# Small experts in shared passes of the array: raw float32 weights on two or four column tiles

## The chip, the cores and the metric

The kernel runs on one core of a Trainium2 chip. The metric is the device time of one execution in microseconds. Inside a profile, times are counted from the first instruction of the span.

## What is computed

Two transformer blocks follow one another on 256 tokens of width 1024, all in float32. The second ends in a mixture of 64 experts, and only that part is touched here. A router picks 8 experts for each token; an expert multiplies its tokens by a gate and an up matrix, and the product of both by a down matrix:

```python
def expert_block(args):
    x_b, g_b = args
    hg = jnp.einsum('td,edf->tef', x_b, w_gate)      # 1024 -> 256, for each expert
    hu = jnp.einsum('td,edf->tef', x_b, w_up)
    return jnp.einsum('tef,efd->td', jax.nn.silu(hg) * hu * g_b[..., None], w_down)
```

An expert has 6 blocks of 128 x 1024 numbers (512 KB): 4 of gate and up together, 2 of down.

## The kernel before

`moe` first computes the router and the shared expert, then orders the experts by their number of tokens (rank 0 has most). It works on 50 ranks; what is beyond their slots is left to a branch behind the outputs (`tc.If`), entered only if a count in `more` is over its limit. The 16 ranks up to `HEAVY` get 128 token slots each; the 34 up to `LIGHT` come in pairs with 64 slots each. One heavy rank or one pair is a unit, and `run` goes through 33 units, heavy and light in turn, two units to a group. The instruction order of SP, TensorE, VectorE and ScalarE is that of the program text.

For a unit u, `run` does this in order:

- Four or eight steps of gate/up, each with one block. In between TensorE turns the result h of the unit before (`turn`), gathers tokens of the next group by products with one-hot matrices (`gather`, tile pga, copied to xg by ScalarE), and makes the tables of a later group (`select`, `tables`, tile pv).
- `swiglu` on ScalarE and VectorE.
- `combine` of unit u - 2: its output, split in two parts, times a one-hot matrix, into four accumulators.
- The down product of unit u - 1 (`dn_block`), with float32 weights just as they were loaded. For a pair the two experts have 64 columns of the array each.

In gate/up a number is the sum of two float32r parts. `load` brings a block into one of 13 raw buffers, taken in turn; ScalarE makes its high part and VectorE the low part (`split`), in six pairs of buffers, and the raw buffer is free again. A heavy unit uses 3 products per chunk of 128 inputs (`gu_block`). A pair uses `gu_block2`: an expert's 64 slots stand twice in xg, high parts above low ones, so that the array holds one expert with both parts stacked, and 2 products per chunk give halves that `swiglu` adds. So the two experts of a pair go through the array one after the other.

`ahead` traces loads so that four gate/up blocks lie ahead of the products; SP issues them in that order, each when its raw buffer is free.

Of the kernel before, what the change touches and what calls it, by code (L numbers as in the profile page):

```python
# [11 lines left out]
F32 = mybir.dt.float32  # L12
# [120 lines left out]
def norm_rows(e, pool, x, g, out):  # L133
    """out = x * rsqrt(mean(x^2) + eps) * g for [128, 1024] (g on all partitions)."""
# [8 lines left out]
def block1_mix(e, a, x, begin):  # L143
    """a: dict of APs; x: two [128, 1024] residual tiles, updated in place; begin()(t, half) is told when a part is done."""
# [20 lines left out]
    # q, k of the neighbourhood attention, transposed: [2 heads x 64, tokens]  # L165
# [13 lines left out]
    def moving(blks, width, per):  # L179
        """Columns with the tokens on partitions: psum tiles for the two halves."""  # L180
# [16 lines left out]
    def attention(pair, q_of, k_of, v_of, bias_of, dst):  # L197
        """Two heads: softmax(q k^T / 8 + bias) v, as [2 x 64, tokens]."""
# [63 lines left out]
    # q, k, v of the grouped attention  # L262
# [17 lines left out]
    for tt, qk in enumerate(qks):  # L280
# [4 lines left out]
        # rotation: halves of 16 within each section of 32  # L285
# [28 lines left out]
    # gates  # L314
# [39 lines left out]
    for nh in range(2):  # L354
# [6 lines left out]
        else:  # L361
            # the first tokens' sums end before the second's
# [30 lines left out]
    # window [r2, c, h, v, c']: rpb[h, v + 5 - r2, c' - c + 15]  # L393
# [33 lines left out]
def peer_norm(e, a, x, s):  # L427
    """The norm of x, transposed in s.xT: returns the function that takes on half of x[t]."""
# [25 lines left out]
def peer(e, a, x, s, side, after, finish):  # L454
    """side(): work of a later part to trace between the last experts; after(): buffers; finish(tail, load) what comes after all but
    the last products, which tail(t, half) does for a part of x.

    x += product-key experts of rmsnorm(x); every expert's row is used densely, gated by G."""
# [10 lines left out]
    # constants  # L469
# [7 lines left out]
    # queries, scores, the best 16 keys of each half  # L477
# [33 lines left out]
    def route():  # L511
# [11 lines left out]
        # the best 16 sums of each head: only pairs (a, b) with (a + 1)(b + 1) <= 16 can be among them  # L523
        for tt in range(2):
# [30 lines left out]
            # expert numbers of the chosen pairs  # L555
# [14 lines left out]
            # gates  # L570
# [67 lines left out]
    def mix(steps, side, share):  # L638
        """Trace the steps with work of the side queue between them, share us of it per step."""
# [68 lines left out]
    # the first tokens' sums end before the second's  # L708
# [75 lines left out]
def norm_mod(e, pool, x, A, sh, out):  # L784
    """out = x * rsqrt(mean(x^2) + eps) * A + sh."""
# [4 lines left out]
def mixer_constants(e, a, m):  # L790
    """What the start of the mixer needs."""
# [12 lines left out]
    # lower bounds: softmax over the two rows, first row  # L804
# [18 lines left out]
def mixer_start(e, a, x, m, tail, load_w):  # L823
    """x += the last sums, x = rmsnorm(x) * gf, the modulated norm of that, transposed, in m.hT, and HGRN2's f in m.pf."""
# [63 lines left out]
    # what the mixer loads next, four blocks ahead of the products  # L888
# [24 lines left out]
def mixer(e, a, x, m):  # L913
    """x += g1 * token_mixer(h) for the h in m.hT."""
# [32 lines left out]
    def moving(blks, src, lhs, name="pmv", per=4):  # L947
        """The tokens on partitions; per blocks at a time for one half of the tokens and then the other."""
# [49 lines left out]
    def conv_all(starts):  # L998
        """Each one's end after the next one's start."""
# [8 lines left out]
    # ---- HGRN2's f; beta and the log decay of each head, tokens on partitions; k  # L1008
# [23 lines left out]
    # softplus(z) = max(z, 0) - ln(sigmoid(|z|))  # L1032
# [38 lines left out]
    # ---- gated delta rule over the whole sequence  # L1071
# [6 lines left out]
    def delta():  # L1078
# [44 lines left out]
        # R = (I + N)^-1 for the strictly upper N, by doubling the inverted blocks  # L1123
# [125 lines left out]
    # ---- outputs, gated  # L1249
# [11 lines left out]
    # from here on the order of the trace is the order of each engine  # L1261
# [66 lines left out]
def turned(e, h, q, tt, dst_hi, dst_lo):  # L1328
    """Four chunks of h from q on, transposed and rounded; returns what traces the low parts."""
# [8 lines left out]
def out_block(e, m, tt, i):  # L1338
    """A block of the output projection, of w_out's columns in m.w into m.po."""
# [43 lines left out]
NE = 64  # L1383
HEAVY = 16
LIGHT = 50
# [28 lines left out]
def moe(e, a, x, m, late, out):  # L1414
    """x += the rest of the mixer's output; out = rms_norm(x + g2 * moe(modulated norm of x)) * final_norm_w."""
# [7 lines left out]
    def add_to(t, p, n, g):  # L1423
        """x += g * p for a column half."""
# [5 lines left out]
    # ---- the rest of the mixer's output projection, the norm, the shared expert's first product, the router  # L1430
# [61 lines left out]
    # silu(x wg) * (x wu) * gate, times wd, of 128 tokens of an expert, or of 64 each of two  # L1492
# [7 lines left out]
    def gu_block2(pg, xx, b, w):  # L1500
        """Rows 64 and on have the tokens' low part."""
        for k in range(2):
            c = 2 * b + k
            s = slice(k * 512, (k + 1) * 512)
            for r in range(2):
                nc.tensor.matmul(pg, xx[:, c], w[r][:, s], start=c == 0 and r == 0, stop=c == NC8 - 1 and r == 1)  # L1506

    def swiglu(pg, gt=1.0):
        h = wk.tile([P, 256], F32, tag="eh", name=uid(e, "hh"))
        if len(pg) == 2:  # L1510
            s = wk.tile([P, 512], F32, tag="t5", name=uid(e, "hs"))
# [4 lines left out]
        else:  # L1516
            s = pg[0]
        nc.scalar.activation(h, s[:, :256], AF.Silu)
        nc.vector.scalar_tensor_tensor(h, h, gt, s[:, 256:], op0=OP.mult, op1=OP.mult)
# [19 lines left out]
    # ---- shared expert, routing  # L1539
# [60 lines left out]
    hsh.append(turn(swiglu([pg[0]])))  # L1600
# [379 lines left out]
```

## Time and profile before

| | |
|---|---|
| runs | 1849.41 us median of 3 (1847.86 to 1853.87) |
| span of the profiled execution | 1846.2 us |
| its own time | not listed beside its span |
| mean granted TensorE clock | 0.981 |
| PE, DVE, ACT, POOL busy | 94%, 77%, 55%, 10% |
| HBM read | 385.74 MB |

The span is the time from the first to the last instruction of one execution. Matmuls are pipelined and their ends are modelled, so that the distance between the starts of two products says more than the length of one.

### The profile page before, as it was taken

To read this page: it belongs to the slowest core of one execution; us is meant where nothing else is said; L and a number is where in the kernel's file an instruction comes from. 1 tells how busy PE (TensorE), PEld (TensorE's weight loads), DVE (VectorE), ACT (ScalarE), POOL (GpSimd) and SP (SyncE) were. 2 spreads that over 40 slices of the span, in tenths; PEclk is the share of its full clock that TensorE was granted. 3 is DMA by queue.
4 is the path that set the end of the run, shared out by engine and by line. 5 is a ranking of instruction groups with operands and counts; after the bars stand their busy time and mean duration, and the time that the engine had idled before them with its cause. 6 is when DMAs were issued, how large, how long until landed. Compare 5 with 4: busy or idle time off the path is not lost.

```text
span 1846.2 us, 30513 instructions
## 1 busy us (share of the span) xinstructions
PE 1739.2 (94%) x11079; PEld 1461.8 (79%) x11079; DVE 1416.0 (77%) x2574; ACT 1023.9 (55%) x1782; POOL 192.5 (10%) x95
## 2 busy tenths in 40 slices
PE   7989898999999999998999989989889999999996
PEld 6779797999899998877777779878667776777774
DVE  5675799986889999777777676886767777877766
ACT  3556454444444444554544555564467777777774
POOL 1030001232111221000000020240200000000000
PEclk9999999999999999999999999999999999999998
DMA  6323544455445555788888554320478988989884
GB/s 232 115 92 127 171 149 156 153 186 169 139 137 162 172 173 170 241 276 283 275 270 278 178 171 144 130 92 1 141 297 303 364 312 320 353 317 354 320 317 186
DMA packets 107551, 388.87 MB, mean 211 GB/s; under 512 B 12592, under 2 KB 12880, under 8 KB 107264
## 3 DMA queue, kind: packets, MB, share of 16 engines
q1 hardware_dynamic: 105552, 382.48, 59.1%
q0 software_dynamic: 976, 2.82, 0.5%
q8 instruction: 89, 1.46, 0.3%
q10 hardware_dynamic: 864, 1.53, 0.3%
q14 instruction: 70, 0.57, 0.1%
HBM read 385.74 MB, written 1.05 MB: 210 GB/s over the span
## 4 chain that ended last, share of the span: by engine, by line
PE 65%; DVE 17%; DMA 10%; ACT 4%; issue 3%; POOL 0%; DVEq 0%; SPq 0%; ACTq 0%
PE acc L682 7%; PE pgu L1506 7%; PE py L1534 7%; DMA raw<-in_w_ada 6%; PE pgu L1498 5%; PE pu L80 5%; PE pu L82 5%; PE pu L81 5%; DVE wlo L67 4%; PE py L1777 3%; PE pga L1761 3%; DMA raw<-in_peer_v 2%; ACT whi L66 2%; PE pg L628 2%; PE pmv L81 1%
## 5 line engine op out<-in xcount | busy, mean ns | idle before, releaser
L66 ACT ACTIVATE whi<-raw 128x1024 fp32r<-128x1024 f32 x537 | 565.8, 1067 | 359.2 <-PE pu L81 141.3
L67 DVE TENSOR_TENSOR wlo<-raw,whi 128x1024 fp32r<-128x1024 f32 x481 | 589.1, 1234 | 159.0 <-ACT whi L66 136.8
L82 PE MATMUL pu<-pxT,wlo 128*128 128x256 f32 x1024 | 290.7, 284 | 10.1 <-DVE wlo L67 7.3
L682 PE MATMUL acc<-whi,hh 128*128 128x512 f32 x1008 | 281.9, 397 | 13.5 <-DVE hh L67 11.0
L80 PE MATMUL pu<-pxT,whi 128*128 128x256 f32 x1024 | 293.4, 286 | 0.7 <-ACT whi L66 0.7
L81 PE MATMUL pu<-pxT,whi 128*128 128x256 f32 x1024 | 290.2, 283 | 0.0
L682 PEld LDWEIGHTS acc<-whi,hh 128*128 128x128 f32 x1008 | 187.1, 188 | 64.8 <-DVE hh L67 20.9
L67 POOL TENSOR_TENSOR wlo<-raw,whi 128x1024 fp32r<-128x1024 f32 x56 | 151.6, 2710 | 661.9 <-ACT whi L66 658.5
L82 PEld LDWEIGHTS pu<-pxT,wlo 128*128 128x128 f32 x1024 | 196.6, 192 | 12.0 <-DVE wlo L67 8.9
L80 PEld LDWEIGHTS pu<-pxT,whi 128*128 128x128 f32 x1024 | 196.6, 192 | 0.9 <-ACT whi L66 0.9
L81 PEld LDWEIGHTS pu<-pxT,whi 128*128 128x128 f32 x1024 | 196.7, 192 | 0.0
L682 PE MATMUL acc<-wlo,hh 128*128 128x512 f32 x504 | 157.2, 392 | 3.0 <-DVE wlo L67 3.0
L66 ACT ACTIVATE hh<-H 128x256 fp32r<-128x256 f32 x126 | 52.5, 417 | 145.4 <-PE acc L682 144.7
L1534 PE MATMUL py<-raw,th 128*64 128x512 f32 (+1 forms) x348 | 117.0, 598 | 1.5 <-ACT xg L1768 0.9
L682 PEld LDWEIGHTS acc<-wlo,hh 128*128 128x128 f32 x504 | 94.9, 189 | 24.0 <-DVE wlo L67 3.8
L1506 PE MATMUL pgu<-whi,xg 128*128 128x512 f32 x272 | 109.2, 401 | 0.0
L1506 PE MATMUL pgu<-wlo,xg 128*128 128x512 f32 x272 | 106.9, 393 | 0.0
L1768 ACT ACTIVATE xg<-pga 128x128 fp32r<-128x128 f32 (+1 forms) x400 | 95.9, 335 | 15.2 <-PE pga L1761 12.9
L762 DVE SCALAR_TENSOR_TENSOR ada<-raw,cs,ada 128x1024 f32<-128x1024 f32 x48 | 61.6, 1284 | 55.3 <-DMA raw<-in_w_ada 55.2
L1498 PE MATMUL pgu<-whi,xg 128*128 128x512 f32 x256 | 94.9, 421 | 1.9 <-ACT whi L66 1.9
L1761 PE MATMUL pga<-S,hs 128*128 128x256 f32 (+1 forms) x544 | 85.8, 286 | 0.0
L1761 PEld LDWEIGHTS pga<-S,hs 128*128 128x128 f32 x544 | 78.6, 190 | 7.2
(579 smaller groups left out, 3298.6 us busy)
## 6 DMA issues: line engine op xcount, KB each, us to landing
raw<-in_w_gu SPq DMA_DIRECT2D x171, 512.0 KB, 6.5
raw<-in_peer_u SPq DMA_DIRECT2D x128, 512.0 KB, 3.6
raw<-in_peer_v SPq DMA_DIRECT2D x128, 512.0 KB, 4.6
raw<-in_w_dn SPq DMA_DIRECT2D x83, 512.0 KB, 8.1
raw<-in_w_ada SPq DMA_DIRECT2D x48, 512.0 KB, 4.4
ada<-in_w_gu SPq DMA_DIRECT2D x29, 512.0 KB, 6.8
raw<-in_w_in_a SPq DMA_DIRECT2D x24, 512.0 KB, 3.5
raw<-in_w2a SPq DMA_DIRECT2D x17, 512.0 KB, 4.3
```

The costliest lines, as they stand in the source:

```text
L66: e.nc.scalar.activation(hi, src, AF.Copy)
L67: (eng or e.nc.vector).tensor_sub(lo, src, hi.bitcast(F32))
L80: nc.tensor.matmul(out, lh, rh, start=first, stop=False)
L81: nc.tensor.matmul(out, lh, rl, start=False, stop=False)
L82: nc.tensor.matmul(out, ll, rh, start=False, stop=last)
L682: nc.tensor.matmul(acc[tt][n], h[l][:, s], w[r][:, n * 512:(n + 1) * 512], start=j == order[0] and i == 0, stop=j == order[-1] and i == 2)
L762: nc.vector.scalar_tensor_tensor(mod[n], w, cs[:, c:c + 1], mod[n], op0=OP.mult, op1=OP.add)
L1498: nc.tensor.matmul(pg, l[:, c], w[r][:, s], start=c == 0 and j == 0, stop=c == NC8 - 1 and j == 2)
L1506: nc.tensor.matmul(pg, xx[:, c], w[r][:, s], start=c == 0 and r == 0, stop=c == NC8 - 1 and r == 1)
L1534: nc.tensor.matmul(py[q][t], th[:, k, t], w[i][:, q * 512:(q + 1) * 512], start=k == 0, stop=last and k == 1)
L1761: nc.tensor.matmul(p[:, k, :m], hs[i][:, tt, s], S[:, tt].rearrange("p u n -> p (u n)")[:, :m], start=tt == 0, stop=tt == 1)
L1768: nc.scalar.activation(t, p[:, :, o:o + P // n], AF.Copy)
```

## The change

- `MID` = 30: the ranks 16 to 29 come in 7 pairs with 64 slots each, the ranks 30 to 49 in 5 fours with 32 slots each. With 16 heavy units that makes 28 units. Heavy units form groups of two, and pairs and fours form groups of two (pair and four, five times, then two pairs); `sorted` mixes both kinds of group.
- Gate/up of pairs and fours takes the raw float32 blocks, without a split: `gu_shared` gives each expert of the unit its own columns of the array (64 or 32) and its own rows of one accumulator. xg holds these tokens once, as float32: `gather` adds up both parts in the accumulator.
- A step of such a unit takes 2 or 4 blocks, one per expert, and the order of loads within a unit goes by block and then by expert.
- `swiglu` has one accumulator and adds no halves. `select` is one comparison per unit. `tables` multiplies each expert's slots by float32 numbers of its own (V has no parts any more).
- The branch behind the outputs has one case more.

```diff
+MID = 30
-    def gu_block2(pg, xx, b, w):
+    def gu_shared(pg, xx, b, ws):
+        n = P // len(ws)
         for k in range(2):
             c = 2 * b + k
-            s = slice(k * 512, (k + 1) * 512)
-            for r in range(2):
-                nc.tensor.matmul(pg, xx[:, c], w[r][:, s], start=c == 0 and r == 0, stop=c == NC8 - 1 and r == 1)
+            for i, w in enumerate(ws):
+                t = slice(i * n, (i + 1) * n)
+                nc.tensor.matmul(pg[t], xx[:, c, t], w[:, k * 512:(k + 1) * 512], start=c == 0, stop=c == NC8 - 1)
...
     def swiglu(pg, gt=1.0):
-        if len(pg) == 2:
-            s = wk.tile([P, 512], F32, tag="t5", name=uid(e, "hs"))
-            nc.scalar.activation(s[:64], pg[0][64:], AF.Copy)
-            nc.scalar.activation(s[64:], pg[1][:64], AF.Copy)
-            nc.vector.tensor_add(s[:64], s[:64], pg[0][:64])
-            nc.vector.tensor_add(s[64:], s[64:], pg[1][64:])
...
-    V = pool.tile([P, 2, NE // 2, 6], F32R, name="V")
+    V = pool.tile([P, 2, NE, 2], F32, name="V")
...
-                    order += [(which, k, r) for r in units[v][0] for k in range(n)]
+                    order += [(which, k, r, len(units[v][0]) > 1) for k in range(n) for r in units[v][0]]
...
-                ready.append(load(src[bass.ds(v + b, 1)].rearrange("o p n -> (o p) n"), which == 1))
+                ready.append(load(src[bass.ds(v + b, 1)].rearrange("o p n -> (o p) n"), which == 1 or shared))
-        def weights():
-            taken[0] += 1
-            return ready[taken[0] - 1]
+        def weights(n):
+            while len(ready) < taken[0] + n:
+                ahead(len(ready) - taken[0] + 1)
+            taken[0] += n
+            return ready[taken[0] - n:taken[0]]
...
-                for i, r in enumerate(ranks):
-                    for tt in range(2):
-                        nc.vector.tensor_scalar(S[:, tt, u, i * n:(i + 1) * n], io1[:, base:base + n],
-                                                pos[:, tt, r:r + 1], None, op0=OP.is_equal)
+                nc.vector.tensor_tensor(S[:, :, u].rearrange("p t (r s) -> p t r s", r=n),
+                                        io1[:, None, None, base:base + P // n].to_broadcast([P, 2, n, P // n]),
+                                        pos[:, :, r:r + n, None].to_broadcast([P, 2, n, P // n]), op=OP.is_equal)
...
-                    nc.tensor.matmul(pv[:, u], S[:, tt, u], V[:, tt, ranks[0] // 2], start=tt == 0, stop=tt == 1)
+                    for i, r in enumerate(ranks):
+                        t = slice(i * w, (i + 1) * w)
+                        nc.tensor.matmul(pv[t, u], S[:, tt, u, t].bitcast(F32), V[:, tt, r], start=tt == 0, stop=tt == 1)
...
+            if len(us[0][0]) == 1:
+                c, i = 2 * (q // 2), q % 2
+                for k in range(2):
+                    pick(k, c + k, [i])
+                nc.scalar.activation(xg[:, c:c + 2, :n, i], p[:, :, :n], AF.Copy)
+            else:
+                pick(0, q, range(2))
+                nc.scalar.activation(xg[:, q, :n], p[:, 0, :n], AF.Copy)
...
-            steps = 4 * len(ranks)
-            for b in range(steps):
+            for b in range(4):
                 if u < len(units):
-                    if len(ranks) == 1:
-                        gu_block(pg[0], xx[:, :, :P], xx[:, :, P:], b, weights())
+                    if n == 1:
+                        gu_block(pg, xx[:, :, 0], xx[:, :, 1], b, *weights(1))
                     else:
-                        gu_block2(pg[b // 4], xx[:, :, b // 4 * P:(b // 4 + 1) * P], b % 4, weights())
+                        gu_shared(pg, xx, b, weights(n))
...
+    one, two, four = shared_by(1, 0, HEAVY, 0), shared_by(2, HEAVY, MID, 0), shared_by(4, MID, LIGHT, 0)
+    mixed = [u for k in range(len(two)) for u in (two[k:k + 1] + four[k:k + 1])]
+    kinds = [[us[i:i + 2] for i in range(0, len(us), 2)] for us in (one, mixed)]
+    order = sorted(((j + 0.5 - 0.2 * k) / len(gs), g) for k, gs in enumerate(kinds) for j, g in enumerate(gs))
+    units = [u for _, g in order for u in g]
     run(units, psh)
```

## Rows read from the trace of the kernel before

**Rows 1.** The page, part 1: busy time of each engine.

```profile
PE 1739.2 (94%) x11079; PEld 1461.8 (79%) x11079; DVE 1416.0 (77%) x2574; ACT 1023.9 (55%) x1782; POOL 192.5 (10%) x95
```

**Rows 2.** Busy time by engine, window of the routed experts; then clock, DMA share, GB/s.

```profile
1351.88:1830.30 478.42, 473.42 (x2246) 338.66 (x2246) 348.34 (x498) 355.30 (x758) 0.00 (x0) 1.00 0.85 325
```

**Rows 3.** The chain that ended last, in order of time: start, length, what.

```profile
1482.19 2.04 PE pgu L1506 x8
...
1492.22 1.97 PE py L1777 x8
...
1507.11 3.58 PE py L1534 x16
1510.69 2.04 PE pgu L1506 x8
...
1539.19 2.04 PE pgu L1506 x8
...
1826.69 3.63 PE py L1534 x16
```

**Rows 4.** Windows of 10 us among the experts, columns as in rows 2.

```profile
1355.00:1365.00 10.00, 7.88 (x32) 5.83 (x32) 5.86 (x5) 7.81 (x21) 0.00 (x0) 0.83 1.03 413
...
1405.00:1415.00 10.00, 10.00 (x43) 7.05 (x43) 9.10 (x15) 7.15 (x14) 0.00 (x0) 1.00 1.02 411
...
1475.00:1485.00 10.00, 10.00 (x52) 6.30 (x51) 5.93 (x8) 6.25 (x16) 0.00 (x0) 1.00 0.56 193
```

**Rows 5.** Waits of SP's queue, 1345 to 1800: total, times, longest.

```profile
SPq L1401 <- PE py L1534: 192.0, 34, 9.7
```

**Rows 6.** TensorE in order of time, first unit: start, length, idle before.

```profile
1351.88 0.48 PE L1498 MATMUL pgu<-whi,xg 128*128 128x512 f32 x1
...
1356.35 0.49 PE L1498 MATMUL pgu<-whi,xg 128*128 128x512 f32 x1 [1.89 <-ACT whi L66]
1357.61 0.80 PE L1498 MATMUL pgu<-wlo,xg 128*128 128x512 f32 x1 [0.76 <-DVE wlo L67]
```

**Rows 7.** TensorE in order of time, start of a light unit's gate/up.

```profile
1510.62 0.50 PE L1506 MATMUL pgu<-whi,xg 128*128 128x512 f32 x1
1510.96 0.40 PE L1506 MATMUL pgu<-wlo,xg 128*128 128x512 f32 x1
1511.20 0.39 PE L1506 MATMUL pgu<-whi,xg 128*128 128x512 f32 x1
1511.43 0.40 PE L1506 MATMUL pgu<-wlo,xg 128*128 128x512 f32 x1
```

**Rows 8.** TensorE in order of time: down products of two light units.

```profile
1480.31 0.59 PE L1534 MATMUL py<-raw,th 128*64 128x512 f32 x1
1480.32 0.59 PE L1534 MATMUL py<-ada,th 128*64 128x512 f32 x1
1480.74 0.59 PE L1534 MATMUL py<-raw,th 128*64 128x512 f32 x1
...
1506.48 0.63 PE L1777 MATMUL py<-yl,St 128*128 128x512 f32 x2
1507.04 3.65 PE L1534 MATMUL py<-raw,th 128*64 128x512 f32 x16
```

**Rows 9.** TensorE in order of time: table products and what follows.

```profile
1491.72 0.50 PE L1739 MATMUL pv<-V,S 128*128 128x6 f32 x4
1492.08 0.71 PE L1777 MATMUL py<-yh,St 128*128 128x512 f32 x2
```

**Rows 10.** Groups by line and shape, from 1200 on: count, busy us, mean ns.

```profile
L67 DVE TENSOR_TENSOR wlo<-raw,whi 128x1024 fp32r<-128x1024 f32 x182 | 218.7, 1224 | 73.4 <-ACT whi L66 52.1 <-PE py L1777 13.7 <-DMA raw<-in_w_gu 1.5
L66 ACT ACTIVATE whi<-raw 128x1024 fp32r<-128x1024 f32 x191 | 200.7, 1086 | 5.5 <-DMA raw<-in_w_gu 5.1 <-PE pmv L82 0.3
```

**Rows 11.** SP in order of time: issues of the first experts' blocks.

```profile
1344.14 5.82 SPq L1401 DMA_DIRECT2D raw<-in_w_gu  x8
```

More of the change, by code (lines that the diff above doesn't have):

```diff
@@ L1658, in moe @@
         nc.vector.tensor_scalar(lst[:, k], pl[:, 0], (4.0, 2.0)[k], None, op0=OP.mult)
-    more = pool.tile([1, 4], F32, name="more")
-    nc.vector.tensor_scalar(more[:, 0:1], pl[:, 1, 0:1], -128.0, 0.0, op0=OP.add, op1=OP.max)
-    nc.vector.tensor_scalar(more[:, 1:2], pl[:, 1, HEAVY:HEAVY + 1], -64.0, 0.0, op0=OP.add, op1=OP.max)
-    nc.vector.tensor_copy(more[:, 2:3], pl[:, 1, LIGHT:LIGHT + 1])
-    nc.vector.tensor_reduce(more[:, 3:4], more[:, 0:3], axis=AX.X, op=OP.max)
-    moreu = pool.tile([1, 4], U32, name="moreu")
+    more = pool.tile([1, 5], F32, name="more")
+    for k, (r, n) in enumerate(((0, 128.0), (HEAVY, 64.0), (MID, 32.0), (LIGHT, 0.0))):
+        nc.vector.tensor_scalar(more[:, k:k + 1], pl[:, 1, r:r + 1], -n, 0.0, op0=OP.add, op1=OP.max)
+    nc.vector.tensor_reduce(more[:, 4:5], more[:, 0:4], axis=AX.X, op=OP.max)
+    moreu = pool.tile([1, 5], U32, name="moreu")
     nc.vector.tensor_copy(moreu, more)
@@ L1743, in tables @@
-            for u, (ranks, base) in enumerate(us):
+            for u in range(n):
                 nc.vector.tensor_scalar(St[:, u], iot, sv[:, u, 0:1], None, op0=OP.is_equal)
-                c = 1 + ranks[0] % 2
-                if len(ranks) == 2:
-                    nc.vector.tensor_copy(sv[64:, u, 1:2], sv[64:, u, 2:3])
-                gt.append(sv[:, u, c:c + 1])
-            xg = pool.tile([P, NC8, 2, T], F32R, tag="xg", name=uid(e, "xg"), bufs=2)
-            return S, St, gt, xg, us
+            if len(us[0][0]) == 1:
+                xg = pool.tile([P, NC8, 2, 2, P], F32R, tag="xg", name=uid(e, "xg"), bufs=2)
+            else:
+                xg = pool.tile([P, NC8, 2, P], F32, tag="xg", name=uid(e, "xg"), bufs=2)
@@ L1752, in gather @@
+            return S, St, [sv[:, u, 1:2] for u in range(n)], xg, us
         def gather(g, q):
             S, xg, us = g[0], g[3], g[4]
-            m = len(us) * P
-            c, i = 2 * (q // 2), q % 2
-            p = ps.tile([P, 2, T], F32, tag="att", name=uid(e, "pga"), bufs=e.att_bufs)
-            for k in range(2):
-                s = slice((c + k) * P, (c + k + 1) * P)
-                for tt in range(2):
-                    nc.tensor.matmul(p[:, k, :m], hs[i][:, tt, s], S[:, tt].rearrange("p u n -> p (u n)")[:, :m],
-                                     start=tt == 0, stop=tt == 1)
@@ L1763, in gather, with pick @@
-            for u, (ranks, _) in enumerate(us):
-                n = len(ranks)
-                for j in range(n):
-                    o = u * P + j * 64
-                    t = xg[:, c:c + 2, u].rearrange("p c (s i n) -> p c s i n", s=n, i=2)[:, :, j, i]
-                    nc.scalar.activation(t, p[:, :, o:o + P // n], AF.Copy)
+            n = len(us)
+            p = ps.tile([P, 2, 2, P], F32, tag="att", name=uid(e, "pga"), bufs=e.att_bufs)
+            def pick(k, c, parts):
+                steps = [(i, tt) for i in parts for tt in range(2)]
+                for i, tt in steps:
+                    nc.tensor.matmul(p[:, k, :n].rearrange("p u n -> p (u n)"), hs[i][:, tt, c * P:(c + 1) * P],
+                                     S[:, tt, :n].rearrange("p u n -> p (u n)"), start=(i, tt) == steps[0],
+                                     stop=(i, tt) == steps[-1])
@@ L1798, in run @@
                     todo = [(new, q) for q in range(4 if u > 1 else 0, 8)] if i else [(new, q) for q in range(4)]
-                ranks, xx = units[u][0], cur[3][:, :, i]
-                pg = [ps.tile([P, 512], F32, tag="tr", name=uid(e, "pgu"), bufs=e.tr_bufs) for _ in ranks]
+                n, xx = len(units[u][0]), cur[3][:, :, i]
+                pg = ps.tile([P, 512], F32, tag="tr", name=uid(e, "pgu"), bufs=e.tr_bufs)
             def fetch(n=1):
@@ L1832, in run @@
                 py = down()
-                w = [weights() for _ in range(2 * len(units[u - 1][0]))]
+                n = len(units[u - 1][0])
                 for k in range(2):
-                    dn_block(py, th, k, w[k::2])
+                    dn_block(py, th, k, weights(n))
                 yh = wk.tile([P, D], F32R, tag="yh", name=uid(e, "yh"), bufs=1)
@@ L1865, in final, with shared_by @@
                 nc.sync.dma_start(out[tt * P:(tt + 1) * P, s], o[:, s])
-    heavy = [((r,), 0) for r in range(HEAVY)]
-    light = [((r, r + 1), 0) for r in range(HEAVY, LIGHT, 2)]
-    units = []
-    while heavy or light:
-        units += heavy[:1] + light[:1]
-        heavy, light = heavy[1:], light[1:]
+    def shared_by(n, lo, hi, base):
+        return [(tuple(range(r, r + n)), base) for r in range(lo, hi, n)]
+    one, two, four = shared_by(1, 0, HEAVY, 0), shared_by(2, HEAVY, MID, 0), shared_by(4, MID, LIGHT, 0)
[3 more added lines that the diff above has]
+    units = [u for _, g in order for u in g]
     run(units, psh)
@@ L1879, in moe @@
     if e.overflow:
-        with tc.If(nc.values_load(moreu[:, 3:4], min_val=0, max_val=T) > 0):
-            v = [nc.values_load(moreu[:, k:k + 1], min_val=0, max_val=T) for k in range(3)]
+        with tc.If(nc.values_load(moreu[:, 4:5], min_val=0, max_val=T) > 0):
+            v = [nc.values_load(moreu[:, k:k + 1], min_val=0, max_val=T) for k in range(4)]
+            with tc.If(v[3] > 0):
+                run(shared_by(2, LIGHT, NE, 0))
             with tc.If(v[2] > 0):
-                run([((r, r + 1), 0) for r in range(LIGHT, NE, 2)])
+                run(shared_by(2, MID, LIGHT, 32))
             with tc.If(v[1] > 0):
-                run([((r, r + 1), 64) for r in range(HEAVY, 32, 2)])
+                run(shared_by(2, HEAVY, MID, 64))
             with tc.If(v[0] > 0):
-                run([((r,), P) for r in range(HEAVY)])
+                run(shared_by(1, 0, HEAVY, P))
             final()
```

34 lines of the change are left out of this document (15 added, 19 removed).

## The prediction

> **What bounds the kernel now.** I read the page first: TensorE is busy for 94% of the span, the other engines are not [rows 1]. The change touches only the routed experts, so I cut the span at them. From the first gate/up product (1351.88) to the last down product, 478.4 us pass, in which TensorE is busy for 473.4, VectorE and ScalarE for about 350 each, and the DMA engines for 85% [rows 2]. The chain of waits then shows that the end is set inside this stage by TensorE alone: piece after piece is PE, and the same pair of units, one heavy and one light, comes round every 28.50 us (1482.19, 1510.69, 1539.19) [rows 3]. So TensorE time taken out of a unit comes off the total, until something else is late. What is late next is seen in windows of 10 us: the DMA engines move 411 to 413 GB/s while they have buffers to fill, and are busy for only 0.56 of a window when they have not [rows 4]; SP then waits for down products to give buffers back, 192 us in all [rows 5]. A block of 0.524 MB at 411 GB/s takes 1.276 us, and the 50 experts have 300 blocks, so the weights alone need 383 us. The change doesn't alter a byte of that.
>
> **Price of a unit before.** A light unit: gate/up, gathers and tables from 1482.19 to 1492.22 are 10.03, its combine 1.97, its down product 3.58 (1507.11 to 1510.69): 15.58. A heavy unit has the rest of 28.50: 12.92 [rows 3]. 16 heavy and 17 light give 471.6; the stage took 478.4, so 7 us go, at the start, where TensorE waits 1.89 and 0.76 for a split [rows 6] and the granted clock of a window reads 0.83 [rows 4].
>
> **Gate/up of the light experts.** Removed: 32 float32r products of a light unit, which follow one another at 0.23 us [rows 7]: 7.4. Added: raw float32 products on column tiles. The trace has that form in the down products: two tiles of 64 columns with different weights start 0.01 apart, and the next two come 0.43 later; one float32 product is two such instructions [rows 8]. So 8 chunks x 2 x 0.43 = 6.9 for two experts, if two tiles are used. Four tiles of 32 columns stand nowhere in the trace. From below they cost 0.43 for four (all together), from above 1.72 (one after another); two and two would be 0.86. I take 0.43, since the second tile adds nothing in the nearest row, and issue isn't the limit: the tiny table products, load and product, come at 0.07 to 0.09 each, four of them in 0.36 [rows 9]. Then a unit of four has also 6.9, and its down product stays at 3.44 plus a switch. TensorE: Matmul & The Clock Gate (Part 3, Measured speedup vs the span model) in the Trainium skill gives 2.38 times for three column tiles; by an estimate from that, a four would cost 0.54 and the total 13 us more. No row here has three tiles, and the rows for two show no such loss.
>
> **Switches of the array.** Going from 128 columns to 64 and back costs, around one down product: 0.10 before it, 0.14 after its last pair, and 0.11 in the next spacing, together 0.35 [rows 7, 8]. A light unit pays that once now. Afterwards gathers (128 columns) stand between the steps of the same unit, so there are three more excursions, 1.05, and one per group for the tables: 1.2 a unit. Bounds are 0 (hidden in waits) and double. TensorEngine Tiling (Array Packing), Key Properties, in the Trainium skill says that a change of tiling mode drains the engine, which speaks against this change; by that rule the 1.2 stands, and the gaps of 0.10 to 0.14 agree with it.
>
> **Tables.** Before, two products per unit at 0.09. Afterwards each expert has its own, in float32 and so as two instructions: 4 for a heavy unit (0.36), 8 for a pair (0.72), 16 for a four (1.44): +0.18, +0.54, +1.26.
>
> **Number of units.** 34 light experts in 17 pairs become 7 pairs and 5 fours; every light unit has the same gathers, combine and down product whether it holds two or four. That, not the cheaper products, is the gain: 5 units fewer. New prices: heavy 13.1; pair 15.58 - 7.4 + 6.9 + 0.54 + 1.2 = 16.8; four 17.6. Sum 16 x 13.1 + 7 x 16.8 + 5 x 17.6 = 415.2, which is 56.4 under 471.6.
>
> **What I cost at nothing.** 136 splits, 1.09 on ScalarE and 1.22 on VectorE each, the two copies and two additions of the light units' halves, and the smaller gather copies [rows 10]: these engines are at 350 of 478 us now [rows 2], and only the start shows TensorE waiting for them. Without that cover nothing is lost, as all of it is removed or halved. Preparing V and the one comparison per unit of `select` are within a few tenths of what they replace. SP issues a block about every 0.72 (8 in 5.82) [rows 11], under 1.276; the four first blocks of a four each need a new address, at a cost between 0 and one more issue time each, 2.9 in all, hidden as long as blocks are in flight. The tail behind the last unit is unchanged. The reference's routing of its own inputs sends 107 tokens to the busiest expert, 56 to the 17th, 28 to the 31st and none to the 51st, so all slots suffice and the branch behind stays untaken.
>
> **The wait that is added.** A shared step now waits for the DMA of its blocks itself; behind it on TensorE stands everything. And a raw buffer stays held until that product, not only until the split; SP, in order over 13 buffers, waits for it. Blocks come more unevenly: a group of pair and four (M) takes 36 blocks, 45.9 us, while TensorE needs 34.4; a group of two heavy units (O) 12 blocks, 15.3, against 26.2. The order is M O O M O M O M O O M O M O, the last M being two pairs. SP can run ahead by 13 buffers less the two to four in use, some 11 blocks or 14.0 us. M after O O: 45.9 - 14.0 = 31.9, under 34.4: no wait. M after one O: 61.2 for both on the DMA side, 60.6 on TensorE: 0.6. The last M (24 blocks, 30.6 against 33.6) none. Steps take four blocks at a time, so I grant 3 us for all of these. The first M has no lead: its blocks start at 1344.14 [rows 11], 45.9 of DMA bring them to 1390, and the last step's products behind its blocks take some 2; TensorE, from 1351.88, would be through at 1386: 6 late, on top of the 7 at the start.
>
> **Sum.** 415.2 + 7 + 6 + 3 = 431 for 478.4: 47 less. The profiled execution's own time is not listed beside its span of 1846.2; the median of the runs is 1849.4, 3.2 above, and I keep that distance. 1846.2 - 47 + 3.2 gives 1802. Its own range: with switches and tables free, TensorE saves 24 more, but then M and O are bound by DMA (61.2 against 56) and about 10 to 14 remain: 1788. With switches at double price 14 more: 1816.
>
> **Rivals.** (1) *Four tiles overlap only in part*, midway between 0.43 and 0.86: a four has 16 + 8 steps, 24 x 0.215 x 5 = 26 more: 1828. For it: no row of four. Against: rows 8. The estimate from the Trainium skill above is half of that. Chance 0.08. (2) *Two and two*, 0.86: 51.6 more, less some 4 of waits that this hides: 1850, no change. 0.06. (3) *The lead is lost*: raw buffers held by TensorE leave SP too little room. With half of the 14 us, each M behind an O waits about 4.5, and the first as before: 1820 to 1825, 0.09. With none, groups cost the larger side each: 5 x 45.9 + 33.6 + 8 x 26.2 = 473 and 1845 to 1850, 0.03. For it: 192 us of SP's waits for TensorE. Against: those waits cost no end now. (4) *The other side: four tiles run one after another*, 1.72 per step: 24 x 1.29 x 5 = 155 more, less the same 4: 1953. It decides from 0.82 per step on, where 24 x 5 x (0.82 - 0.43) eats the 47. 0.04. (5) *The clock falls*: in the window of the start where TensorE waited, the granted clock was 0.83 of 2.4 GHz, part of it so at 1.2 [rows 4]. If the first M runs at 1.2, its 34.4 become 69, 23 over the 46 that DMA takes: 1825, 0.03; if every M does, over 100 us, slower, 0.03. Against: the stage as a whole reads 1.00. (6) The change doesn't take effect as built, or another wait takes all: 0.02, no change.
>
> **Chances.** The forecast has 0.62. Faster by over 0.3% (5.5 us, about what separates the runs shown): 0.62 + 0.08 + 0.09 + 0.03 = 0.82. Within: (2), (3) without lead and (6), 0.11. Slower: (4) and half of (5), 0.07. A range from 1785 to 1838 leaves out (2), (4), the lead lost whole and the clock lost in every M, and holds the rest, some 0.8.
>
> **What would show it.** Products of `gu_shared` in a four: four starts within 0.05 us, next four 0.43 later; 0.86 or 1.72 kills the sum. A pair's unit near 16.8 and a four's near 17.6 on the chain. Stage 431 us from the first gate/up product to the last down product. The DMA share over it at about 0.93, with waits of TensorE for raw blocks mostly in the first 45 us; waits of several us in each M mean rival 3. The granted clock in M at 1.00. No second run behind the outputs.

## The result, and the profile after

The changed kernel takes 1857.94 us (median of 15, 1850.81 to 1862.74) where the kernel before takes 1847.97 beside it: a ratio of 1.0064, interval 1.0049 to 1.0079. It is slower by some 10 us; 1802 was forecast. The profiled span is 1860.3 us.

The page, part 1, of the changed kernel, answers to [rows 1]:

```profile
PE 1707.9 (92%) x11067; PEld 1376.2 (74%) x11067; DVE 1210.9 (65%) x2273; ACT 833.4 (45%) x1304; POOL 192.5 (10%) x95
```

TensorE, VectorE and ScalarE are all busy for less time, and the end comes later. So I cut at the experts again, as in [rows 2, 4]: the stage, and windows of 10 us in it (length, then busy time of PE, PEld, DVE, ACT, POOL, then granted clock, DMA share, GB/s).

```profile
1351.98:1844.40 492.42, 442.37 (x2210) 252.90 (x2209) 144.14 (x210) 166.38 (x285) 0.00 (x0) 0.94 0.83 317
1370.00:1380.00 10.00, 9.43 (x51) 3.57 (x50) 0.00 (x0) 2.66 (x5) 0.00 (x0) 1.00 1.02 407
...
1400.00:1410.00 10.00, 5.75 (x20) 5.13 (x21) 3.68 (x3) 5.02 (x8) 0.00 (x0) 0.51 0.62 248
...
1500.00:1510.00 10.00, 2.51 (x12) 1.89 (x13) 0.78 (x1) 1.87 (x4) 0.00 (x0) 0.77 1.03 410
1510.00:1520.00 10.00, 10.00 (x54) 6.75 (x57) 4.51 (x5) 4.00 (x7) 0.00 (x0) 0.72 0.13 51
```

The stage takes 492.4 us, not 431. TensorE now stands idle for 50 of them, where it stood for 5; VectorE and ScalarE are busy for 144 and 166. From 1500 to 1510 almost nothing runs but DMA; in the next 10 us TensorE is full, at a granted clock of 0.72, and DMA does almost nothing (51 GB/s). Bound by transfers in one window and leaving them idle in the next: that is a queue which stops and goes.

TensorE's waits in the stage (total, times, longest), then ScalarE's on its splits, then SP's, which answers to [rows 5]:

```profile
PE pga L1755 <- ACT th L1522: 33.8, 7, 7.5
```

```profile
ACT whi L66 <- DMA raw<-in_w_gu: 49.8, 24, 9.2
ACT whi L66 <- DMA ada<-in_w_gu: 24.9, 6, 9.9
```

```profile
SPq L1403 <- PE py L1529: 144.3, 30, 14.8
```

Seven times TensorE waits for the small copy `th` on ScalarE, an engine that is busy for a third of the stage. What ScalarE does then is seen in its instructions in order of time (start, length, what, idle time before):

```profile
1508.13 1.06 ACT L66 ACTIVATE whi<-ada 128x1024 fp32r<-128x1024 f32 x1 [9.90 <-DMA ada<-in_w_gu]
1509.09 0.36 ACT L1522 ACTIVATE th<-phT 128x256 f32<-128x256 f32 x1
1509.36 0.38 ACT L1766 ACTIVATE xg<-pga 128x256 f32<-128x256 f32 x1
```

A split has waited 9.90 us for its block; `th` and the gather's copy stand behind it and follow at once. The same stretch on TensorE, and SP's issues:

```profile
1501.62 0.40 PE L1500 MATMUL pgu<-whi,xg 128*128 128x512 f32 x1
1509.51 1.22 PE L1755 MATMUL pga<-S,hs 128*128 128x256 f32 x4 [7.49 <-ACT th L1522]
1510.53 0.63 PE L1500 MATMUL pgu<-whi,xg 128*128 128x512 f32 x1
1510.96 0.63 PE L1500 MATMUL pgu<-wlo,xg 128*128 128x512 f32 x1
```

```profile
1487.06 9.29 SPq L1403 DMA_DIRECT2D raw<-in_w_dn  x8
1497.80 1.81 SPq L1403 DMA_DIRECT2D ada<-in_w_gu  x2
...
1502.79 16.58 SPq L1403 DMA_DIRECT2D raw<-in_w_dn  x2
```

So the story of one stall is this. The unit running is the first heavy one after a four. At its first step `ahead` reaches the first gate/up block of the second heavy unit, which stands in the order of loads behind the eight down blocks of the four (8 x 1.276 = 10.2 us of transfer, issued from 1487.06). The block's split is written into ScalarE's program there, ahead of `th` and of the gather's copies. ScalarE waits, TensorE runs out of work at 1502, the products at 1510 come 0.43 apart instead of 0.23, and SP, which waits for the down products, takes 16.58 us for two issues: that is the idle DMA of the window behind. In the kernel before, ScalarE's splits waited 5.1 us for gate/up blocks from 1200 on [rows 10]; here it is 74.7 in the stage alone.

The forecast's prices hold meanwhile. TensorE in order of time, gate/up of a four, answers to [rows 8]:

```profile
1477.55 0.60 PE L1509 MATMUL pgu<-raw,xg 128*32 128x512 f32 x2
1477.56 0.60 PE L1509 MATMUL pgu<-ada,xg 128*32 128x512 f32 x2
1477.98 0.60 PE L1509 MATMUL pgu<-raw,xg 128*32 128x512 f32 x2
1477.99 0.60 PE L1509 MATMUL pgu<-ada,xg 128*32 128x512 f32 x2
```

Four tiles of 32 columns start within 0.01, and the next four 0.43 later. The chain, where nothing is late, answers to [rows 3]:

```profile
1682.90 2.75 PE pgu L1500 x12
...
1695.82 2.75 PE pgu L1500 x12
...
1709.92 3.58 PE pgu L1509 x16
...
1784.81 3.58 PE pgu L1509 x16
...
1789.24 1.87 PE pgu L1509 x8
...
1800.08 3.58 PE pgu L1509 x16
...
1815.50 2.95 PE pgu L1500 x12
```

A heavy unit takes 12.92 (forecast 13.1), a pair 15.27 and 15.42 (16.8); tables of a later group come on top where they stand, as in the heavy unit from 1695.82, which takes 14.10. A four and the heavy unit behind it, in the stall told above, read on the same chain:

```profile
1475.45 1.98 PE pgu L1509 x16
...
1495.26 2.55 PE pgu L1500 x11
...
1520.74 2.92 PE pgu L1500 x12
```

The four takes 19.8 (forecast 17.6) and the heavy unit 25.5 (13.1): the greater part of the loss lies behind the four.

### The profile page after: what moved, and what is told of

The parts are those of the page before. It is cut to its first block, busy times and chain, and to the rows that moved or that the text cites. A ratio compares the mean times of both kernels' runs of the same rounds, so it can differ in the third digit from the quotient of the medians.

```text
span 1860.3 us, 29388 instructions
## 1 busy us (share of the span) xinstructions
PE 1707.9 (92%) x11067; PEld 1376.2 (74%) x11067; DVE 1210.9 (65%) x2273; ACT 833.4 (45%) x1304; POOL 192.5 (10%) x95
## 3 DMA queue, kind: packets, MB, share of 16 engines
HBM read 385.74 MB, written 1.05 MB: 208 GB/s over the span
## 4 chain that ended last, share of the span: by engine, by line
PE 60%; DVE 16%; DMA 16%; ACT 4%; issue 3%; POOL 0%; SPq 0%; DVEq 0%; ACTq 0%
PE acc L682 7%; DMA raw<-in_w_ada 5%; PE py L1529 5%; PE pu L80 5%; PE pu L81 5%; PE pu L82 5%; DMA raw<-in_w_gu 5%; PE pgu L1500 4%; DVE wlo L67 4%; PE pgu L1509 3%; DMA raw<-in_peer_v 3%; PE py L1775 3%; PE pga L1755 2%; ACT whi L66 2%; DMA ada<-in_w_gu 2%
## 5 line engine op out<-in xcount | busy, mean ns | idle before, releaser
L66 ACT ACTIVATE whi<-raw 128x1024 fp32r<-128x1024 f32 x418 | 439.9, 1056 | 405.0 <-PE pu L81 141.2
L67 DVE TENSOR_TENSOR wlo<-raw,whi 128x1024 fp32r<-128x1024 f32 x362 | 447.9, 1240 | 169.1 <-ACT whi L66 164.6
L1755 PEld LDWEIGHTS pga<-S,hs 128*128 128x128 f32 x448 | 65.4, 206 | 63.3 <-ACT th L1522 37.7
L1755 PE MATMUL pga<-S,hs 128*128 128x256 f32 x448 | 77.7, 310 | 34.7 <-ACT th L1522 33.8
L1509 PE MATMUL pgu<-raw,xg 128*32 128x512 f32 (+1 forms) x464 | 102.8, 600 | 3.2 <-DMA raw<-in_w_gu 3.2
L1529 PE MATMUL py<-raw,th 128*32 128x512 f32 (+2 forms) x360 | 99.4, 598 | 0.8 <-ACT th L1522 0.5
L1500 PE MATMUL pgu<-whi,xg 128*128 128x512 f32 x256 | 96.3, 429 | 0.0
L67 DVE TENSOR_TENSOR yl<-py,yh 128x512 fp32r<-128x512 f32 x56 | 38.2, 690 | 77.6 <-ACT yh L66 77.6
L66 ACT ACTIVATE yh<-py 128x512 fp32r<-128x512 f32 x56 | 32.9, 597 | 91.7 <-PE py L1529 91.7
```

The source lines that it names most:

```text
L66: e.nc.scalar.activation(hi, src, AF.Copy)
L67: (eng or e.nc.vector).tensor_sub(lo, src, hi.bitcast(F32))
L1500: nc.tensor.matmul(pg, l[:, c], w[r][:, s], start=c == 0 and j == 0, stop=c == NC8 - 1 and j == 2)
L1509: nc.tensor.matmul(pg[t], xx[:, c, t], w[:, k * 512:(k + 1) * 512], start=c == 0, stop=c == NC8 - 1)
L1529: nc.tensor.matmul(py[q][t], th[:, k, t], w[i][:, q * 512:(q + 1) * 512], start=k == 0, stop=last and k == 1)
L1755: nc.tensor.matmul(p[:, k, :n].rearrange("p u n -> p (u n)"), hs[i][:, tt, c * P:(c + 1) * P], S[:, tt, :n].rearrange("p u n -> p (u n)"), ...
```

## The experiments

Theory A: the blocked queue, as just told. Theory B, the third rival: the lead of the transfers (the blocks that have landed ahead of their products) is lost, since 13 raw buffers held until the products leave SP too little room. Each ratio is to the kernel before, timed beside it. That kernel's median lay between 1845.5 and 1850.0 from one group of runs to another, so a gain taken from two groups is good to some 5 us; gains in the text are differences of medians.

| run | edit to the changed kernel | median us | ratio (interval) |
|---|---|---|---|
| e1 | look ahead 3 blocks | 1840.71 | 0.9954 (0.9941 to 0.9967) |
| e2 | look ahead 2 blocks | 1834.98 | 0.9931 (0.9905 to 0.9957) |
| e3 | four ahead of pair | 1874.84 | 1.0148 (1.0117 to 1.0179) |
| e4 | 17 raw pairs, no fours | 1865.14 | 1.0083 (1.0055 to 1.0112) |
| e5 | those splits on VectorE | 1828.17 | 0.9876 (0.9841 to 0.9912) |
| e6 | those blocks loaded earlier | 1820.56 | 0.9841 (0.9812 to 0.9871) |
| e7 | e6 and e1 | 1823.17 | 0.9850 (0.9815 to 0.9885) |
| e8 | 11 raw buffers | 1879.70 | 1.0158 (see below) |
| e9 | heavy groups first | 1855.45 | 1.0037 (1.0015 to 1.0058) |
| e10 | e6 and e9 | 1825.13 | 0.9870 (0.9834 to 0.9906) |
| e11 | e6 with 40 transfers fewer | 1778.27 | 0.9641 (0.9604 to 0.9677) |
| e12 | e10 and e5 | 1827.45 | 0.9883 (0.9844 to 0.9922) |
| e13 | e6 with 15 raw buffers | 1810.33 | 0.9807 (0.9780 to 0.9834) |
| e14 | 15 raw buffers alone | 1843.57 | 0.9979 (0.9959 to 0.9998) |

**e1 and e2: how far the splits are written ahead.**

```diff
-AHEAD = 4
+AHEAD = 3        # e2: 2
```

> Loads are traced three gate/up blocks ahead of the products in place of four. SP's order and the buffers stay the same; what moves is the place of the splits among ScalarE's other work: the split of the second heavy unit's first block, which waits for the eight down blocks of a four, now stands behind the copy of the turned h (th) and one gather copy, not ahead of them. Theory A (ScalarE's queue is blocked at its head by a split that waits for a transfer, and TensorE waits for the copies behind it): TensorE's waits for th, 33.8 us in 7 times, go to under 5, some come back behind gather copies; 15 to 30 us faster than the changed kernel, about 1830 to 1843. Theory B (the lead is lost, TensorE is short of weights because raw buffers are held until its products): SP's order and buffers are as before, so within 5 us of the changed kernel, about 1858.

> Two gate/up blocks ahead. The waiting split now stands behind th and both kinds of gather copy of a heavy unit's third step. Theory A: 35 to 50 us faster than the changed kernel, about 1808 to 1823, if a split two steps ahead is still early enough (a step of a heavy unit with its gathers takes 1.4 to 2.3 us, the two halves of a split 1.06 and 1.23). Theory B: within 5 us of the changed kernel.

17 and 23 us come back, in e2 less than A expected. In e1 the waits for `th` are gone, and TensorE waits for gather copies one step later instead; in e2 the stall is later still, and splits that are now too late are added. TensorE's largest waits of e1, then of e2:

```profile
PE pga L1755 <- ACT xg L1766: 19.5, 3, 7.2
PE pga L1755 <- ACT xg L1763: 11.8, 2, 6.0
```

```profile
PE py L1529 <- ACT xg L1766: 10.6, 3, 4.3
PE pgu L1500 <- DVE wlo L67: 10.2, 17, 0.8
```

So the place of the split in ScalarE's program moves the stall, as A says.

**e3: the four ahead of the pair.**

```diff
-    mixed = [u for k in range(len(two)) for u in (two[k:k + 1] + four[k:k + 1])]
+    mixed = [u for k in range(len(two)) for u in (four[k:k + 1] + two[k:k + 1])]
```

> Within a mixed group the four comes ahead of the pair, so that four down blocks (5.1 us) instead of eight (10.2 us) stand ahead of the second heavy unit's first block. Theory A: each of the five stalls of 8 to 10 us shrinks by about 5 us: 20 to 30 us faster than the changed kernel, about 1830 to 1838. Theory B: the group has the same 36 blocks and the same products, so within 5 us.

My expectation from A was wrong in sign. TensorE's largest wait of e3:

```profile
PE pv L1735 <- ACT xg L1763: 48.9, 7, 10.4
```

The four's down blocks now lie ahead of the first heavy unit's gate/up blocks, whose first split is written at the pair's third step: the same blocked head, in front of the copies of another gather. Moving the four doesn't avoid a split behind its down blocks.

**e4: raw columns, but no fours.**

```diff
-MID = 30
+MID = 50
...
```

> One part alone: raw float32 weights in their own columns for 17 pairs, no fours (MID = 50, the lone pair last). A pair's unit without waits took 15.3 to 15.4 us in the trace of the changed kernel, against 15.58 of a light unit before, so TensorE's sum is 16 x 12.95 + 17 x 15.4 = 469, as before. A group of two pairs takes 24 blocks, 30.6 us, and TensorE 30.8. Theory A: four down blocks stand ahead of the waiting split, so stalls of at most 2 to 3 us at eight transitions: 1846 to 1865. Theory B: transfers are well under TensorE's need, nothing to wait for: 1844 to 1849.

With 17 raw pairs (the last one alone) and the overflow case of the fours gone from the branch behind the outputs, the chain is TensorE nearly throughout. Two heavy units and two pairs in it:

```profile
1448.54 2.95 PE pgu L1500 x12
...
1476.09 3.58 PE pgu L1509 x16
...
1507.84 2.96 PE pgu L1500 x12
```

They come round in 59.3 us, of which the pairs take 31.75, where two heavy and two stacked pairs took 57.0 [rows 3]. The run is 17 us slower than the kernel before, about what theory A had at the most and more than B. So raw columns bring nothing by themselves: what is gained below is the gain of units saved, as the forecast had it.

**e5: the blocked splits off ScalarE.** The gate/up blocks of the second heavy unit behind each four (20 blocks) have both parts made by VectorE.

```diff
+        if eng == "dve":
+            e.nc.vector.tensor_copy(hi, t)
+            e.nc.vector.tensor_sub(lo, t, hi.bitcast(F32))
...
+                    late = v > 1 and len(units[v][0]) == 1 and len(units[v - 2][0]) == 4
...
```

> The changed kernel, but both halves of the splits of the 20 blocks that come behind a four's down blocks (the second heavy unit after a four) are done by VectorE, so that ScalarE has nothing in its queue that waits for those transfers. Loads, their order and buffers are untouched. Theory A (ScalarE's queue blocked at its head): TensorE's waits for th (33.8 us in 7 times) go to under 3, the clock stays at 1.00 there, 30 to 45 us faster than the changed kernel, about 1813 to 1828. Theory B (TensorE short of weights, the lead lost): the same waits come back under another name, within 5 us of the changed kernel, about 1858.

No load and no buffer is changed, and 30 us come back. The waits for `th` are gone; TensorE's largest wait of e5 is for VectorE, whose queue now has the same split at its head:

```profile
PE phT L1524 <- DVE yl L67: 20.3, 11, 3.2
```

**e6 and e7: the blocked blocks loaded earlier.** The gate/up blocks of that heavy unit go ahead of the four's down blocks in the order of loads; the order of use stays.

```diff
+        late = [u for u in range(1, len(units) - 1) if len(units[u - 1][0]) == 4 and len(units[u + 1][0]) == 1]
+        for u in range(len(units) + 1):
+            if u - 1 not in late:
+                order += blocks_of(0, u)
+            if u in late:
+                order += blocks_of(0, u + 1)
+            order += blocks_of(1, u - 1)
```

> Only the order of loads is changed: the gate/up blocks of the second heavy unit after a four come ahead of the four's eight down blocks. The split that blocked ScalarE waits 10.2 us less; the down blocks come 5.1 us later and TensorE may wait for them. Theory A: of each of the five stalls of 8 to 10 us some 5 to 8 go: 20 to 40 us faster than the changed kernel, about 1818 to 1838. Theory B: the same blocks in the same time, within 5 us.

> Both remedies at once, the order of e6 and loads traced three blocks ahead. Theory A: they remove the same stall, so no more than 10 us beyond the better of the two alone: 1810 to 1830. Theory B: about as e1, 1841.

37 us come back, the waits for `th` are gone, and a shorter look ahead (e7) adds nothing to that. The granted clock of the stage reads 1.00 again. What is left in e6 is another matter. Its chain in order of time, around a four:

```profile
1463.32 3.57 PE pgu L1509 x32
...
1469.03 9.26 DMA ada<-in_w_dn
...
1478.40 10.10 DMA raw<-in_w_gu
...
1488.62 10.12 DMA raw<-in_w_dn
...
1498.78 1.90 PE py L1529 x10
```

Three batches of blocks follow one another on the DMA engines and end at a down product: TensorE waits for supply there. The stage takes 455 us from the first gate/up product to the last down product. Not all of that wait is idle time. TensorE in order of time, fourth step of the same four:

```profile
1470.18 1.48 PE L1509 MATMUL pgu<-raw,xg 128*32 128x512 f32 x4
1471.90 1.04 PE L1509 MATMUL pgu<-raw,xg 128*32 128x512 f32 x2 [0.24 <-DMA raw<-in_w_gu]
1473.20 1.90 PE L1509 MATMUL pgu<-raw,xg 128*32 128x512 f32 x10 [0.25 <-DMA raw<-in_w_gu]
```

The blocks of its experts land one after another, and their column tiles run one after another; the step takes 4.85 us up to the next gather (1475.03), where the step before took 1.86 (1467.65 to 1469.51). Only 0.49 of that reads as idle.

**e8: two raw buffers less.**

```diff
-RAW1 = 3
+RAW1 = 1
```

> The changed kernel with 11 raw buffers in place of 13 (RAW1 = 1): two blocks, 2.6 us, less lead for each of the five groups of pair and four. Theory B: each of them waits 2.6 us more, 10 to 15 us slower than the changed kernel, about 1870. Theory A: the stall is set by the order in ScalarE's queue, not by the lead: within 5 us, about 1858.

Eight down blocks of a four and four gate/up blocks of the second heavy unit are traced ahead of the four's first down product. That is 12 blocks on 11 buffers, so one is loaded over before its product has read it, and part of the products use other weights. Its time rests on that too, and I conclude nothing from it.

**e9 and e10: heavy groups first, without and with e6.**

```diff
-    order = sorted(((j + 0.5 - 0.2 * k) / len(gs), g) for k, gs in enumerate(kinds) for j, g in enumerate(gs))
+    order = sorted(((j + 0.5 + 0.2 * k) / len(gs), g) for k, gs in enumerate(kinds) for j, g in enumerate(gs))
```

> The changed kernel with another order of the groups alone: O M O M O O M O M O M O O M, a group of heavy units first and the two pairs last. The blocked split of theory A stays at all five transitions from a four to heavy units. Theory A alone: no change but the start, where the first M no longer stands without lead, 5 to 10 us less: about 1848 to 1853. Theory B (what matters is how evenly the blocks are asked for): 15 to 25 us less, about 1833 to 1843.

> The order of loads of e6 (1820.6) and the order of groups of e9. Theory A is already served by e6, so beyond it only the start gains: 5 to 10 us, 1810 to 1816. Theory B: the rest of e6's loss, 24 us of stage over the forecast, is lead, and more of it goes: 1798 to 1810.

The first mixed group then has a heavy group in front of it in which SP could build a lead. e9 gains some 2.5 us (5 by the ratios), near nothing, and e10 nothing beyond e6; both miss what either theory expected. The lead isn't lost at the start alone: in e10 the first four, now behind heavy units, takes 20.2 us, as late as the others.

**e11: is the rest of e6 supply?** The second of two gate/up blocks of each expert in a four reads the block before it again, so 40 of the 300 transfers are left out, and those products use other weights. All products and copies stay.

```diff
+            if which == 0 and b % 2 and o[4] == 0 and MID <= r < LIGHT:
+                ready[o] = ready[(0, b - 1, r, shared, 0)]
...
+                return
```

> e6 with 40 of the 300 transfers left out: every second gate/up block of a four is the block before it once more, so these experts are computed with half of their gate and up weights. TensorE does the same products. If what e6 still loses is supply (51 us of transfers less, group of pair and four 28 blocks, 35.7 us, near TensorE's 30.7): 25 to 50 us under e6, 1770 to 1796. If it is again an order in some engine's queue: within 10 us of e6, 1810 to 1821.

42 us go (37 by the ratios), of the 51 (40 x 1.276) that the transfers took. With the transfers their buffers are saved too, so this run doesn't tell the bytes from the lead. The chain is nearly all TensorE; here it is over a pair, a four, two heavy units:

```profile
1494.27 3.58 PE pgu L1509 x16
...
1509.56 3.57 PE pgu L1509 x32
...
1519.71 0.64 PE pv L1762 x24
...
1525.98 2.95 PE pgu L1500 x12
...
1540.06 2.95 PE pgu L1500 x12
...
1547.89 1.05 PE pv L1762 x8
...
1554.37 1.00 PE pgu L1509 x3
```

The four units take 60.1 us, where the forecast had 60.6 (16.8 + 17.6 + 2 x 13.1), a four alone 16.4. The stage takes 412.3 (1347.73 to 1760.0); the forecast had 415.2 for TensorE's units and 7 more for the start.

**e12: both ways around the blocked queue.** e10 with the splits of e5.

> e10, and the splits of the second heavy unit after a four by VectorE as in e5. Theory A: the order of loads already took the blocked split away, so within 5 us of e10. If ScalarE is still blocked in e10, 5 to 10 us less than e10.

Nothing beyond e10: the two cures remove one thing.

**e13 and e14: two raw buffers more, with and without e6.** One pair of split buffers makes room for them.

```diff
-RAW0 = 4
+RAW0 = 6
...
-    load = wide_load(e, [(early, RAW0), (e.stage, e.raw_bufs)], [(early, 4), (e.stage, e.w_bufs)])
+    load = wide_load(e, [(early, RAW0), (e.stage, e.raw_bufs)], [(early, 3), (e.stage, e.w_bufs)])
```

> e6 with 15 raw buffers in place of 13; their room comes from one of the six pairs of split buffers. If the supply that e6 still lacks is a matter of lead (SP waits 88 us for down products to give buffers back): up to two blocks, 2.6 us, more for each group of pair and four that follows heavy units: 5 to 12 us under e6, 1808 to 1816. If the transfers of such a group are too many whatever the lead, or the split buffers now bind: within 4 us of e6 or slower.

> The changed kernel with 15 raw buffers and five pairs of split buffers. Theory B (the lead): 5 to 12 us under the changed kernel, about 1848. Theory A (the blocked split in ScalarE's queue sets the stall): within 4 us, about 1858; TensorE's waits for th stay at 30 to 35 us.

e13 is 36 us under the kernel before, the fastest run whose products all use their own weights, and faster than both kernels. It is 10 us under e6, but only 6 by the ratios, whose intervals touch; in the profiled stages it is 10.6 (444.5 against 455.1). Of the 15 us between the profiled spans of e6 and e13, 4.5 lie ahead of the stage (first gate/up product at 1346.01 instead of 1350.49). e14 is 14 under the changed kernel although its waits for `th` stay, so A alone, which allowed some 4, doesn't explain it. TensorE's largest wait of e14:

```profile
PE pga L1755 <- ACT th L1522: 33.7, 5, 7.6
```

**Where the time goes, unit by unit.** A unit's time is counted in the traces from its first gate/up product to that of the next unit. e11 has the same products and waits for next to nothing, so what a unit takes beyond its time in e11 is time lost by waits or by the clock (us in the stage, of the profiled executions):

| run | stage | first pair and four | four later fours | first heavy units behind a four | second ones |
|---|---|---|---|---|---|
| changed kernel | 492.5 | 6.0 | 12.9 | 56.6 | 4.7 |
| e5 | 463.8 | 6.0 | 12.4 | 8.7 | 24.4 |
| e6 | 455.1 | 5.9 | 13.1 | 23.9 | 0.0 |
| e13 | 444.5 | 6.1 | 0.7 | 25.5 | 0.0 |
| e14 | 473.6 | 5.7 | 0.9 | 54.8 | 0.0 |

All other units take the same time in these runs, within 0.1 us in sum. So two things are lost in different places. The blocked queue sits in the heavy units behind a four, where e6 gives back 37 us and two more buffers alone (e14) only 6.5. The waits of the fours for their own gate/up blocks, 13 us, don't change with the queue and go with two more buffers.

## Why the prediction was wrong

It had the gain right, left out a queue and put the late blocks too low, point by point:

- **What bounds the kernel** and **the gain comes from fewer units**: right. Without the late blocks and 40 transfers the stage takes 412 us (e11), and without the fours nothing is gained (e4).
- **Four tiles at 0.43 per step**: right, against rivals 1, 2 and 4: two steps of a four are 3.57 on the chain of e11, eight times 0.43 and 0.13 for a switch. The Trainium skill's figure for three column tiles (2.38 times; TensorE: Matmul & The Clock Gate, Part 3, Measured speedup vs the span model) would have made this 0.54, by an estimate. The trace doesn't show that loss.
- **Switches at 1.2 a unit**: too dear. A pair's step of two chunks is 1.87 on the chain, four times 0.43 and 0.15, so three excursions cost some 0.45. The rule that a change of tiling mode drains the engine (the Trainium skill, TensorEngine Tiling (Array Packing), Key Properties) is borne out by gaps of that size, and no more.
- **Tables**: too dear for pairs and fours, too cheap for heavy units. The 24 products of a pair and a four take 0.64 on the chain of e11, where 2.16 stood; the 8 of two heavy units take 1.05, where 0.72 stood. With that and the switches a pair and a four come out 1.5 and 1.2 under their forecasts there, and two heavy units 2.2 over theirs (28.4 against 26.2). That the sum of the four units holds to 0.5 is luck.
- **What I cost at nothing: the splits**. This is the step that failed. I priced them by the load of ScalarE and VectorE, "at 350 of 478 us now", and less of it afterwards. Their load did fall, to 166 and 144. But a split is also a wait for a transfer, standing in a queue that runs in program order, and the change put the eight down blocks of a four in front of one of these transfers. Cured by another engine (e5) or by another order of loads (e6), it gives back 30 and 37 us, and both cures together no more (e12).
- **The wait that is added**: right in kind, and much too low. TensorE's idle time before these products is 3.9 us in all (`pgu L1509 <- DMA`), but that isn't what late blocks cost. By the units, those of the first group cost 6 us, as forecast, and those of the later fours 13. As the fourth step of a four in e6 shows, column tiles that run one after another fill the time and count as busy. What I didn't ask is what stands behind the waiting split on ScalarE.
- **The lead, 14 us, and 3 us for all later late blocks**: the second term that failed. With the queue cured 37 us of late blocks are left in e6 beside the 6 at the start: 13 in the fours, and 24 in the heavy units behind them, which end at the down products of the four. The count of 11 blocks took those on their way for ready ones: by their landing times in the trace of the changed kernel, 12 blocks were issued when a four began, and 8 or 9 had landed. Besides, a pair and a four take TensorE 31.7 us without waits (e11), not 34.4, so the 31.9 that the transfers need after the lead leave no room. Two buffers more remove the 13 (e13, e14), but not the 24.
- **Rival 3, the lead lost**: right in part. Its case of half the lead (1820 to 1825) is near e6 (1820.6), that is, near what is left when the queue is cured. Even its worst case (1845 to 1850) lies under the 1858 measured.
- **Rival 5, the clock falls**: true as a consequence. The stage reads 0.94, with 0.51 in the window of a stall. Of the 80 us between the 492 here and the 412 of e11, 47 are idle TensorE, and 33 are busy time that the same products took longer (442 instead of 409). The clock explains about half of that: by the trace's clock records 35 of the 442 us are at 1.2 GHz, so some 18 us are lost, by an estimate. Column tiles that run one after another can make up the rest: e6 is busy for 438 us with the granted clock at 1.00.
- **Sum.** The forecast's 431 had 422 for TensorE and the start, 6 for the first group and 3 for the later late blocks. Measured, the first is 412 (e11), the second 6, the third 37 (e6); with 37 more for the queue, these make the 492 of the changed kernel. So the miss of 61 (56 in the medians) would have been 10 us greater if TensorE's part had not come out lower.
- **Small slips**: switches and tables together are 27 us, not "24 more" (16 x 0.18 + 7 x 1.74 + 5 x 2.46), which moves no bound of the range; and the rows give 0.09 for a table product, not "0.07 to 0.09".

Open: why the 24 us in the heavy units behind the fours stay with two more buffers. In e6 they are near the 5 x 5.1 by which the new order moves the down blocks back, but e5, which moves none, loses 8.7 and 24.4 in the same units. e11 removes them by leaving out transfers and with them buffers held, and no run takes the two apart.

## What to carry to other kernels

An instruction that costs its engine little can cost much by where it stands: for each instruction that waits for a transfer, count the transfers in front of it after the change, and list what follows it on its engine, not only on the busiest one. When units become larger, the blocks that lie between two units of the other kind become larger too, so the order of loads and the number of buffers have to be looked at anew. Where one kind of work no longer needs a step (here the split), the other kind still does, and the look ahead written for an even mix no longer fits it.

## What the hardware showed

- Four column tiles of 32 with float32 weights run as fast as two of 64 ([rows 8]): the next instructions start 0.43 later, for all of them together.
- After an idle stretch of 7.49 us products that had come 0.23 apart came 0.43 apart: the granted clock was 0.77 in the window of the idle stretch and 0.72 in the next, part of either at 1.2 GHz.
- The DMA engines moved 407 GB/s in a window in which a four's products read raw blocks (1370 to 1380), and 410 in one in which almost nothing else ran (1500 to 1510). Before it was 411 to 413 [rows 4].
